# Loading and contracting the first two batches of a batched matmul one by one on all 128 rows

## Chip, cores and metric

One core of a Trainium2 chip. The metric is the time of one execution on the device, in microseconds (us). Each kernel is run several times beside the kernel before on the same chip. A ratio is the mean time of one kernel's fast runs over the mean of the other's fast runs of the same rounds, so it is not quite the ratio of the medians quoted beside it; brackets give its 95% interval. A run counts as slow when it is over 1.5% above the fastest of the same kernel. "MiB complete at t" in my own tables is summed from the packet records of a trace (start, duration and size of each DMA packet), with t counted from the start of the span.

Words used below: PE is TensorE with its matmuls, PEld its loading of weights, DVE is VectorE, ACT is ScalarE, SPq is the issuing of DMAs by SyncE. The span is the profiled execution from its first to its last instruction. A run of bytes is a stretch that lies together in memory; each is moved as one packet. A DMA has landed when the last of the 16 DMA engines has delivered its share. The turn is the moment near 80 us at which the queue goes over from loads to outputs.

## The reference

```python
def setup_inputs():
    batch, m, k, n = 16, 512, 512, 512
    return {"a": np.random.randn(batch, k, m).astype(np.float32),
            "b": np.random.randn(batch, k, n).astype(np.float32)}

def reference(a, b):
    return np.matmul(a.transpose(0, 2, 1), b).astype(np.float32)
```

Sixteen products of 512 x 512 matrices. 33.6 MB are read and 16.8 MB written.

## The kernel before

Batches are taken in pairs. The two batches of a pair lie one above the other in the 128 partitions: partitions 0 to 63 hold batch 0, 64 to 127 batch 1, each partition eight rows of k, so one load is 2 MB in 16 KB runs. Each matmul contracts 64 rows; the two batches run side by side in the two row groups of the array.

```python
G = 2; Q = P // G; R = K // Q; V = 2; RV = R // V; T = M // P; H = T // 2; pairs = batch // G
in_v = [x.rearrange("(pair g) (q r) m -> pair (g q) r m", g=G, r=R) for x in (a, b)]
NX = 4                                    # input buffers of 2 MB
x_ts   = [pool.tile([P, R, M], f32) ...]  # NX of them
abf_ts = [pool.tile([P, RV, M], bf) ...]  # V of them; bbf_ts the same
# ... cut ...
for n in range(2 * pairs):                # SyncE: all loads, then all outputs, one queue
    if n >= NX:
        nc.sync.wait_ge(s_in, n - NX + 1) # a buffer is free when both halves are cast
    nc.sync.dma_start(x_ts[n % NX][:], in_v[n % 2][n // 2]).then_inc(s_x[n % NX], 16)
for i in range(pairs - 1):
    nc.sync.wait_ge(s_out, i + 1)
    nc.sync.dma_start(out_v[i], o_ts[i % NO][:]).then_inc(...)

for i in range(pairs):                    # VectorE: f32 -> bf16, in two halves v
    for v in range(V):
        if i and v == 0: nc.vector.wait_ge(s_v, G * i)
        if i and v == 1: nc.vector.wait_ge(s_mm, G * H * i)
        for n in (2 * i, 2 * i + 1):
            if v == 0: nc.vector.wait_ge(s_x[n % NX], 16 * (n // NX + 1))
            nc.vector.tensor_copy(out=(bbf_ts if n % 2 else abf_ts)[v][:],
                                  in_=x_ts[n % NX][:, v * RV:(v + 1) * RV, :]).then_inc(s_cast, 1)
            if v == V - 1:
                nc.vector.memset(dve_done[:, n:n + 1], 0.0).then_inc(s_in, 1)

with nc.tensor.Fori(0, pairs):            # TensorE
    for v in range(V):
        nc.tensor.wait_ge(s_cast, 2).then_inc(s_cast, -2)
        for t in range(T):
            # ... wait for a free PSUM tile; cut ...
            for r in range(RV):
                for g in range(G):
                    rows = slice(g * Q, (g + 1) * Q)
                    # matmul of 64 rows into ps_ts[g][h]; cut
# ScalarE copies PSUM to o_ts and marks the pair for output; cut
```

Of the kernel before, what the change touches and what calls it, by code (L numbers as in the profile page):

```python
# [1 line left out]

# [4 lines left out]

@with_exitstack
def kernel(
    ctx: ExitStack,  # L10
    tc: tile.TileContext,
    a: bass.AP,
    b: bass.AP,
    out: bass.AP,
):
    nc = tc.nc
    P = 128
    batch, K, M = a.shape
    _, _, N = b.shape
    f32 = mybir.dt.float32  # L20
    bf = mybir.dt.bfloat16




    G = 2
    Q = P // G
    R = K // Q
    V = 2
    RV = R // V  # L30
    T = M // P
    H = T // 2
    pairs = batch // G
    in_v = [x.rearrange("(pair g) (q r) m -> pair (g q) r m", g=G, r=R) for x in (a, b)]
    out_v = out.rearrange("(pair g) (c t) n -> pair c g t n", g=G, t=T)

    NX = 4
    NO = pairs - 1



    pool = ctx.enter_context(tc.tile_pool(name="sb", bufs=1))
    psum = ctx.enter_context(tc.tile_pool(name="ps", bufs=1, space=bass.MemoryType.PSUM))


    done = pool.tile([1, 96], f32, name="done")
    dve_done, act_done = done[:, 0:2 * pairs], done[:, 2 * pairs:3 * pairs]
    x_ts = [pool.tile([P, R, M], f32, name=f"x{j}") for j in range(NX)]
    abf_ts = [pool.tile([P, RV, M], bf, name=f"abf{v}") for v in range(V)]
    bbf_ts = [pool.tile([P, RV, N], bf, name=f"bbf{v}") for v in range(V)]  # L50
    o_ts = [pool.tile([P, G, T, N], f32, name=f"o{j}") for j in range(NO)]
    ps_ts = [[psum.tile([P, 2, N], f32, name=f"ps{g}{h}") for h in range(H)] for g in range(G)]

    s_x = [tc.alloc_semaphore(f"s_x{j}") for j in range(NX)]
    s_o0 = tc.alloc_semaphore("s_o0")
    s_o = tc.alloc_semaphore("s_o")
    s_in = tc.alloc_semaphore("s_in")
    s_cast = tc.alloc_semaphore("s_cast")
    s_v = tc.alloc_semaphore("s_v")
    s_mm = tc.alloc_semaphore("s_mm")  # L60
    s_ev = [tc.alloc_semaphore(f"s_ev{h}") for h in range(H)]
    s_out = tc.alloc_semaphore("s_out")

    with tc.tile_critical(no_gpsimd_drain=True):  # L64
        for n in range(2 * pairs):
            if n >= NX:
                nc.sync.wait_ge(s_in, n - NX + 1)
            nc.sync.dma_start(x_ts[n % NX][:], in_v[n % 2][n // 2]).then_inc(s_x[n % NX], 16)
        for i in range(pairs - 1):
            nc.sync.wait_ge(s_out, i + 1)  # L70
            nc.sync.dma_start(out_v[i], o_ts[i % NO][:]).then_inc(s_o if i else s_o0, 16)

        for i in range(pairs):
            for v in range(V):
                if i and v == 0:
                    nc.vector.wait_ge(s_v, G * i)
                if i and v == 1:
                    nc.vector.wait_ge(s_mm, G * H * i)
                for n in (2 * i, 2 * i + 1):
                    if v == 0:  # L80
                        nc.vector.wait_ge(s_x[n % NX], 16 * (n // NX + 1))
                    nc.vector.tensor_copy(  # L82
                        out=(bbf_ts if n % 2 else abf_ts)[v][:],
                        in_=x_ts[n % NX][:, v * RV:(v + 1) * RV, :],
                    ).then_inc(s_cast, 1)
                    if v == V - 1:

                        nc.vector.memset(dve_done[:, n:n + 1], 0.0).then_inc(s_in, 1)  # L88

        for h in range(H):  # L90
            nc.tensor.sem_inc(s_ev[h], 1)
        with nc.tensor.Fori(0, pairs):
            for v in range(V):
                nc.tensor.wait_ge(s_cast, 2).then_inc(s_cast, -2)
                for t in range(T):
                    h = t // 2
                    if v == 0 and t % 2 == 0:
                        nc.tensor.wait_ge(s_ev[h], 1).then_inc(s_ev[h], -1)  # L98
# [3 lines that stand above are left out]
                            a_m = abf_ts[v][rows, r, :].rearrange("p (c t) -> p t c", t=T)  # L102
                            mm = nc.tensor.matmul(  # L103
                                ps_ts[g][h][:, t % 2, :],
                                a_m[:, t],
                                bbf_ts[v][rows, r, :],
                                start=(v == 0 and r == 0),
                                stop=(v == V - 1 and r == RV - 1),
                            )
                            if v == 0 and t == T - 1 and r == RV - 1:  # L110
                                mm.then_inc(s_v, 1)
                            if v == V - 1 and t % 2 and r == RV - 1:
                                mm.then_inc(s_mm, 1)

        for i in range(pairs):
            if i == NO:
                nc.scalar.wait_ge(s_o0, 16)
            for h in range(H):
                for g in range(G):
                    nc.scalar.wait_ge(s_mm, G * H * i + G * h + g + 1)  # L120
                    ev = nc.scalar.copy(  # L121
                        out=o_ts[i % NO][:, g, 2 * h:2 * h + 2, :], in_=ps_ts[g][h][:]
                    )
                ev.then_inc(s_ev[h], 1)

            nc.scalar.memzero(act_done[:, i:i + 1]).then_inc(s_out, 1)  # L126


    with tc.tile_critical(sync_engine=mybir.EngineType.Pool, no_gpsimd_drain=True):
        nc.gpsimd.wait_ge(s_o0, 16)  # L130
        nc.gpsimd.wait_ge(s_o, 16 * (pairs - 2))
    tc.no_sync_barrier()
    nc.sync.dma_start(out_v[pairs - 1], o_ts[(pairs - 1) % NO][:])


# [1 line left out]
_INS = ['a', 'b']  # L137
_OUTS = [((16, 512, 512), 'float32')]


# [23 lines left out]
```

## Time and profile before

| | |
|---|---|
| time, median of the first 3 runs | 123.9 us (123.84 to 124.15) |
| span of the profiled run | 121.9 us |
| PE, VectorE, ScalarE busy | 51%, 31%, 26% of the span |
| DMA queue busy | 97.6% of 16 engines' span |

How to read it: compare the last row with the one above it.

### The profile page before, as it was taken

The page shows a single profiled execution, that of the slowest core. Times are in us where ns is not written, and L with a number is a line of the kernel's source. Part 1 is how long each engine was busy: PE and PEld are TensorE (multiplying, and loading weights), DVE is VectorE, ACT ScalarE, POOL GpSimd, SP SyncE. Part 2 cuts the span into 40 slices and gives each one's busy share as a digit, 9 for nine tenths or more (in the row PEclk, how much of TensorE's full clock was granted, in tenths as well). Part 3 has the DMA queues.
Part 4 walks back from the last instruction along what each step waited for, and adds up shares of the span by engine and source line. Part 5 has one row for each costly group of instructions (what it writes and reads, how often), then busy time and mean ns, then how long its engine had stood idle before and what let it go on. Part 6 is the DMA issues. An engine that isn't in the chain of part 4 may idle for free. (4 is left out here: it accounts for less than half of the span.)

```text
span 121.9 us, 1261 instructions
## 1 busy us (share of the span) xinstructions
PE 62.5 (51%) x512; PEld 35.8 (29%) x512; DVE 38.0 (31%) x48; ACT 31.8 (26%) x41; POOL 0.2 (0%) x4
## 2 busy tenths in 40 slices
PE   0000099989669749969919988946960000000000
PEld 0000044546246314536605645624630000000000
DVE  0003560784194092474356247419000000000000
ACT  4000000480920830190470075091083000000000
POOL 0000000000000000000000000000000000000000
PEclk9999999999999977999995899999999655555555
DMA  5899999999999999999999999999999999999994
GB/s 108 360 430 430 436 430 430 430 430 430 430 430 430 430 430 436 430 430 430 430 430 430 430 430 430 436 390 428 428 430 430 430 428 430 430 430 428 428 428 175
DMA packets 4480, 50.33 MB, mean 413 GB/s; under 512 B 384, under 2 KB 384, under 8 KB 384
## 3 DMA queue, kind: packets, MB, share of 16 engines
q1 hardware_dynamic: 4480, 50.33, 97.6%
HBM read 33.55 MB, written 16.78 MB: 413 GB/s over the span
## 5 line engine op out<-in xcount | busy, mean ns | idle before, releaser
L103 PE MATMUL ps<-bbf,abf 64*128 64x512 bf16 x512 | 62.5, 403 | 27.9 <-PEq L98 27.9
L103 PEld LDWEIGHTS ps<-bbf,abf 64*128 64x128 bf16 x512 | 35.8, 114 | 54.1 <-issue 37.8
L121 ACT COPY o<-ps 128x1024 f32<-128x1024 f32 x32 | 30.1, 1026 | 59.8 <-PE ps L103 59.8
L82 DVE CAST abf<-x 128x2048 bf16<-128x2048 f32 x16 | 19.6, 1224 | 26.6 <-PE ps L103 17.6
L82 DVE CAST bbf<-x 128x2048 bf16<-128x2048 f32 x16 | 19.6, 1225 | 20.8 <-DMA x<-in_b_dram 20.8
L126 ACT ACTIVATE done<-done 1x1 uint32<-1x1 uint32 x8 | 1.6, 196 | 0.0
L121 ACT ACT_TABLE_LOAD x1 | 1.3, 1283 | 0.9 <-SPq L64 0.9
L88 DVE MEMSET done<- 1x1 f32 x16 | 0.9, 59 | 0.0
L148 POOL MEMSET const-bfloat16-1.0<- 128x1 bf16 x1 | 0.1, 101 | 0.0
L148 POOL MEMSET const-uint8-127<- 128x1 uint8 x1 | 0.1, 101 | 0.0
L148 POOL MEMSET const-float32-0.0<- 128x1 f32 x1 | 0.1, 98 | 0.2 <-issue 0.2
L148 POOL MEMSET const-float32-1.0<- 128x1 f32 x1 | 0.1, 98 | 0.0
## 6 DMA issues: line engine op xcount, KB each, us to landing
x<-in_a_dram SPq DMA_DIRECT2D x8, 2048.0 KB, 12.1
x<-in_b_dram SPq DMA_DIRECT2D x8, 2048.0 KB, 15.9
out_dram<-o SPq DMA_DIRECT2D x8, 2048.0 KB, 30.8
```

The lines of the kernel that those rows point to most:

```text
L82: nc.vector.tensor_copy(out=(bbf_ts if n % 2 else abf_ts)[v][:], in_=x_ts[n % NX][:, v * RV:(v + 1) * RV, :],).then_inc(s_cast, 1)
L88: nc.vector.memset(dve_done[:, n:n + 1], 0.0).then_inc(s_in, 1)
L103: mm = nc.tensor.matmul(ps_ts[g][h][:, t % 2, :], a_m[:, t], bbf_ts[v][rows, r, :], start=(v == 0 and r == 0), stop=(v == V - 1 and r == R ...
L121: ev = nc.scalar.copy(out=o_ts[i % NO][:, g, 2 * h:2 * h + 2, :], in_=ps_ts[g][h][:])
L126: nc.scalar.memzero(act_done[:, i:i + 1]).then_inc(s_out, 1)
L148: nc = _bacc.Bacc("TRN2", target_bir_lowering=False, num_devices=1)
```

## The change

The intent: let PE begin sooner. The first two batches are loaded one after the other, each spread over all 128 partitions (four rows of k per partition, 8 KB runs, 1 MB per DMA), so the first batch is there after half the bytes, and it is contracted on all 128 rows with half as many matmuls. All other pairs stay as they were.

```diff
+    in0_v = [x.rearrange("batch (p r) m -> batch p r m", r=RV) for x in (a, b)]
...
-        for n in range(2 * pairs):
+        for u in range(G):
+            for j in range(2):
+                nc.sync.dma_start(
+                    x_ts[j][:, u * RV:(u + 1) * RV, :], in0_v[j][u]
+                ).then_inc(s_x[j] if u else s_f[j], 16)
+        for n in range(2, 2 * pairs):
...
+        for u in range(G):
+            if u:
+                nc.vector.wait_ge(s_mm, H)               # batch 1's casts wait for batch 0's matmuls
+            for j, bf_ts in enumerate((abf_ts, bbf_ts)):
+                nc.vector.wait_ge(s_x[j] if u else s_f[j], 16)
+                nc.vector.tensor_copy(
+                    out=bf_ts[0][:], in_=x_ts[j][:, u * RV:(u + 1) * RV, :]
+                ).then_inc(s_cast, 1)
+                if u == G - 1:
+                    nc.vector.memset(dve_done[:, j:j + 1], 0.0).then_inc(s_in, 1)
...
+                if i == 1 and v == 0:
+                    nc.vector.wait_ge(s_mm, G * H)       # pair 1's casts wait for batch 1's matmuls
...
+        with nc.tensor.Fori(0, G):
+            a_m = abf_ts[0][:].rearrange("p r (c t) -> p r t c", t=T)
+            nc.tensor.wait_ge(s_cast, 2).then_inc(s_cast, -2)
+            for t in range(T):
+                # ... wait for a free PSUM tile; cut ...
+                for r in range(RV):
+                    mm = nc.tensor.matmul(ps_ts[0][h][:, t % 2, :], a_m[:, r, t], bbf_ts[0][:, r, :],
+                                          start=(r == 0), stop=(r == RV - 1))
+                if t % 2:
+                    mm.then_inc(s_mm, 1)
-        with nc.tensor.Fori(0, pairs):
+        with nc.tensor.Fori(0, pairs - 1):
```

(ScalarE's copies of the first pair change their order accordingly.)

More of the change, by code (lines that the diff above doesn't have):

```diff
@@ L54 @@
     s_x = [tc.alloc_semaphore(f"s_x{j}") for j in range(NX)]
+    s_f = [tc.alloc_semaphore(f"s_f{j}") for j in range(2)]
     s_o0 = tc.alloc_semaphore("s_o0")
@@ L71 @@
             nc.sync.dma_start(out_v[i], o_ts[i % NO][:]).then_inc(s_o if i else s_o0, 16)
-        for i in range(pairs):
-            for v in range(V):
-                if i and v == 0:
-                    nc.vector.wait_ge(s_v, G * i)
-                if i and v == 1:
+        for u in range(G):
[8 more added lines that the diff above has]
+                    nc.vector.memset(dve_done[:, j:j + 1], 0.0).then_inc(s_in, 1)
+        for i in range(1, pairs):
+            for v in range(V):
+                if i == 1 and v == 0:
+                    nc.vector.wait_ge(s_mm, G * H)
+                if i > 1 and v == 0:
+                    nc.vector.wait_ge(s_v, G * (i - 1))
+                if i > 1 and v == 1:
                     nc.vector.wait_ge(s_mm, G * H * i)
@@ L91 @@
             nc.tensor.sem_inc(s_ev[h], 1)
-        with nc.tensor.Fori(0, pairs):
+        with nc.tensor.Fori(0, G):
+            a_m = abf_ts[0][:].rearrange("p r (c t) -> p r t c", t=T)
+            nc.tensor.wait_ge(s_cast, 2).then_inc(s_cast, -2)
+            for t in range(T):
+                h = t // 2
+                if t % 2 == 0:
+                    nc.tensor.wait_ge(s_ev[h], 1).then_inc(s_ev[h], -1)
+                for r in range(RV):
+                    mm = nc.tensor.matmul(
+                        ps_ts[0][h][:, t % 2, :],
+                        a_m[:, r, t],
+                        bbf_ts[0][:, r, :],
+                        start=(r == 0),
+                        stop=(r == RV - 1),
+                    )
+                if t % 2:
+                    mm.then_inc(s_mm, 1)
+        with nc.tensor.Fori(0, pairs - 1):
             for v in range(V):
@@ L117 @@
                 nc.scalar.wait_ge(s_o0, 16)
-            for h in range(H):
+            if i == 0:
+                for g in range(G):
+                    for h in range(H):
+                        nc.scalar.wait_ge(s_mm, H * g + h + 1)
+                        nc.scalar.copy(
+                            out=o_ts[0][:, g, 2 * h:2 * h + 2, :], in_=ps_ts[0][h][:]
+                        ).then_inc(s_ev[h], 1)
+            for h in range(H if i else 0):
                 for g in range(G):
```

## The prediction

> **What bounds the kernel now.** I read the page first: the table of busy time, the forty slices, the queue.
>
> ```profile
> PE 62.5 (51%) x512; PEld 35.8 (29%) x512; DVE 38.0 (31%) x48; ACT 31.8 (26%) x41; POOL 0.2 (0%) x4
> ...
> DMA  5899999999999999999999999999999999999994
> GB/s 108 360 430 430 436 430 430 430 430 430 430 430 430 430 430 436 430 430 430 430 430 430 430 430 430 436 390 428 428 430 430 430 428 430 430 430 428 428 428 175
> ...
> q1 hardware_dynamic: 4480, 50.33, 97.6%
> ```
>
> No compute engine is busy for much over half of the span, while the DMA row reads 9 from the third slice to the last but one and GB/s stays at 430. The kernel is one long transfer: 50.33 MB / 430 GB/s = 117.0 us of the 121.9 us span. The rest lies at both ends and at the turn from reading to writing, so I cut those into half microseconds (columns: stretch, length, busy time of the engines, clock, DMA share, GB/s).
>
> ```profile
> 1.50:2.00 0.50, 0.00 (x0) 0.00 (x0) 0.00 (x0) 0.50 (x1) 0.00 (x0) 1.00 0.48 131
> 2.00:2.50 0.50, 0.00 (x0) 0.00 (x0) 0.00 (x0) 0.18 (x1) 0.00 (x0) 1.00 1.74 295
> 2.50:3.00 0.50, 0.00 (x0) 0.00 (x0) 0.00 (x0) 0.00 (x0) 0.00 (x0) 1.00 0.80 164
> 3.00:3.50 0.50, 0.00 (x0) 0.00 (x0) 0.00 (x0) 0.00 (x0) 0.00 (x0) 1.00 0.52 164
> 3.50:4.00 0.50, 0.00 (x0) 0.00 (x0) 0.00 (x0) 0.00 (x0) 0.00 (x0) 1.00 0.69 295
> ...
> 80.50:81.00 0.50, 0.14 (x2) 0.00 (x0) 0.00 (x0) 0.50 (x2) 0.00 (x0) 1.00 0.47 197
> ...
> 120.00:120.50 0.50, 0.00 (x0) 0.00 (x0) 0.00 (x0) 0.00 (x0) 0.00 (x0) 0.50 0.25 98
> ```
>
> Five terms: 1.5 us before the first packet; a ramp from 1.5 to 4.0 us that moves 0.52 MB where 430 GB/s would move 1.07, a loss of 1.28 us; 117.0 us of bytes; 0.27 us lost in the dip at 80.5 us; about 1.7 us from the last packet (120.2) to the end. Sum 121.8, against 121.9 measured. The timed 123.9 us is 2.0 us over the span. No compute appears in the sum. It matters only if it starves the queue, so the next view is the instructions in order of time, first those of the queue's issuer, then those of VectorE and of PE.
>
> ```profile
> 0.94 0.39 SPq L68 DMA_DIRECT2D x<-in_a_dram  x1
> 1.39 0.42 SPq L68 DMA_DIRECT2D x<-in_b_dram  x1
> 1.86 0.42 SPq L68 DMA_DIRECT2D x<-in_a_dram  x1
> 2.32 0.69 SPq L68 DMA_DIRECT2D x<-in_b_dram  x1
> 16.08 0.33 SPq L68 DMA_DIRECT2D x<-in_a_dram  x1
> 17.23 0.33 SPq L68 DMA_DIRECT2D x<-in_b_dram  x1
> 26.07 0.33 SPq L68 DMA_DIRECT2D x<-in_a_dram  x1
> ```
>
> ```profile
> 8.84 1.23 DVE L82 CAST abf<-x 128x2048 bf16<-128x2048 f32 x1 [8.84 <-DMA x<-in_a_dram]
> 13.67 1.23 DVE L82 CAST bbf<-x 128x2048 bf16<-128x2048 f32 x1 [3.60 <-DMA x<-in_b_dram]
> 14.81 1.22 DVE L82 CAST abf<-x 128x2048 bf16<-128x2048 f32 x1
> ...
> 15.19 9.54 PE L103 MATMUL ps<-bbf,abf 64*128 64x512 bf16 x64 [15.19 <-PEq L98]
> ...
> 23.44 1.23 DVE L82 CAST bbf<-x 128x2048 bf16<-128x2048 f32 x1 [0.87 <-DMA x<-in_b_dram]
> ```
>
> The fifth load is issued at 16.08, while the first four still run: b of pair 1 lands only at 23.44. Unhindered, a load lands 2.0 MB / 430 = 4.88 us after the one before it, so the fifth is due at 28.3; the very first load took 8.84 - 0.94 = 7.9 us from issue to landing on an empty queue. Issued by 28.3 - 7.9 = 20.4 it leaves no gap: slack 4.3 us. For the seventh the limit is 20.4 + 9.75 = 30.1; it is issued at 26.07, slack 4.0. These are the quantities on which the change could act. At the other end the last output is issued at 92.71 and the queue runs on to 120.2; compute leads by 27 us there (the issuer's longest wait, 27.8 us, is for the output DMA).
>
> The chain of waits in the page ends at the last ScalarE mark and covers about 7% of the span; it misses the DMA tail, so I do not use it.
>
> **What the Trainium skill says.** "DMA: Bandwidth & Descriptors", section Bandwidth ("Where 436 GB/s comes from"), gives a port ceiling of 435 GB/s for the sixteen engines; the trace agrees with its 430, so there is nothing to win in rate. The same page, "Rules for kernel authors", asks for 128 partitions and at least 1 MiB per DMA; the new loads are just that. "TensorE: Matmul & The Clock Gate", Part 1, says that the array starts at half clock and is released after some 3.4 us of activity. The trace shows it: weight loads come in twos 0.427 us apart from 15.16 to 20.24, and later 64 matmuls take 7.21 us, 0.225 us a pair. Its Part 2 says that a weight load for the next matmul is pulled ahead of the running one if it goes to another row group or to the background weight buffer. The kernel before alternates between two row groups, so its trace cannot tell what full-array loads will do; that is my main uncertainty below.
>
> **The change, part by part.**
> Loads. Two 2 MB loads become four of 1 MB, in 8 KB runs instead of 16 KB. Bytes are the same. Each DMA carries 16 tiny packets (the page has 384 under 512 B for 24 DMAs), so packets go from 4480 to 1792 + 512 for inputs, 2048 for outputs and 26 x 16 = 416 small ones: 4768. If the whole gap from 435 to 430 (1.1% of 117 us, 1.35 us) were the price of 24 DMAs, one would cost 0.056 us, and two more 0.1 us. Outputs already go in 8 KB runs, at 430 GB/s from 93 to 105 us, so the shorter run should cost no rate. Two more issues of about 0.45 us lie before the data that they fetch is needed. Net: 0 to +0.1 us.
>
> First compute. Half of each 2 MB comes 2.44 us sooner: a of batch 0 at 8.84 - 2.44 = 6.4, b of batch 0 at 8.84, a and b of batch 1 at 11.3 and 13.7. PE starts 1.52 us after the b landing (15.19 - 13.67), so at 10.4 instead of 15.2. This gain of 4.8 us is not on the path that sets the end; no output is issued before 66.27 in any case.
>
> New waits. There is only one pair of bf16 buffers for both batches, so the casts of batch 1 wait for all 16 matmuls of batch 0, and the casts of pair 1 wait for all of batch 1. Batch 0: 16 matmuls of 128 rows, about 12 cold at 0.427 (5.1 us of cold clock, as before) and 4 at 0.225: 6.0 us, to 16.4. Cast of a of batch 1 then starts near 16.5, and the fifth load comes 1.27 us later (16.08 - 14.81): 17.8, against the limit of 20.4. Its slack falls from 4.3 to 2.6 us and stays positive. The other cast ends near 19.0, PE restarts at 19.1 and, warm, takes 16 x 0.225 = 3.6 us, to 22.7. Pair 1's casts: a from 22.8, b from 24.0, second a from 25.1, so the seventh load at 26.4 (26.07 before), limit 30.1. PE takes up pair 1 at 25.3 (25.10 before). From there both kernels are alike.
>
> Matmuls fall from 512 to 480, worth some 32 x 0.11 us of PE time in the first pair at most; PE is not on the path. ScalarE copies keep their number and size.
>
> Sum: 121.9 + 0.05 in the span, hence 123.9 timed.
>
> **The rivals.**
> (1) The queue runs dry. If full-array weight loads (0.11 us each in the trace) do not hide, batch 0 takes 1.8 us more and ends at 18.2: fifth load at 19.6, still under 20.4; batch 1 ends at about 26.3 and the seventh load goes at 30.0, right at its limit. If moreover the clock drops in the pause between the batches (2.7 us; the trace shows pauses of 2.3 to 2.7 us, with 64 matmuls in 7.10 after the one at 80.6 to 83.3, so still warm), batch 1 costs another 3 us, and the gap in the queue is about 3 us: 127. Both must hold together; I give that 3%. One alone makes 0 to 0.5 us.
> (2) The earlier start of compute is worth its 4.8 us: 119. It would need compute on the path at the end. The 27 us between the last output's issue and its landing speak against it. 1%.
> (3) The ramp changes. The loss of 1.28 us belongs to the first packets, 16 KB each; packets of 8 KB could shorten or lengthen it by some tenths. Nothing in the profile tells the sign. 123.5 to 124.3.
> (4) Reads in 8 KB runs are slower than writes in 8 KB runs. At 390 GB/s, the rate of the worst full slice, 4.19 MB would take 1.0 us more: 124.9. I see no ground for it.
>
> **Range and chances.** The centre is 123.9. Runs of before spread over 0.3 us, and (3) and a little of (4) add some tenths on either side, more upwards because of (1): 123.5 to 124.5. Over 2% faster means under 121.4, which only (2) gives: 0.01. Over 2% slower means over 126.4, which only the full form of (1) gives: 0.03. Within 2%: 0.96.
>
> **What would show it right or wrong.** Right: GB/s at 430 in every slice from the third to the last but one except near 80 us; 4768 packets; first cast at about 6.4 and first matmul near 10.4 us; fifth load issued near 17.8 and seventh near 26.4; last output issued near 92.7 as before; span within 0.4 us of 121.9. Wrong: a slice near 23 or 33 us with less than 400 GB/s would be rival 1; a first stretch with another shape, rival 3; landings of the first four loads more than 2.44 us apart, rival 4; a last output that lands sooner by as much as compute starts sooner, rival 2.

## The result, and the profile after

Changed kernel 124.14 us (median of 4, 124.02 to 124.19), kernel before 123.92 us (median of 4): ratio 1.0013 [0.9996, 1.0031]. A second set on another occasion gave 123.97 against 124.11, ratio 0.9995 [0.9974, 1.0016]. No difference can be told.

The page of the changed kernel:

```profile
PE 64.9 (53%) x480; PEld 35.8 (29%) x480; DVE 37.9 (31%) x48; ACT 32.1 (26%) x41; POOL 0.2 (0%) x4
...
DMA  2999999999999999999999999999999999999994
GB/s 56 423 429 429 458 429 434 434 429 429 429 429 440 429 434 429 429 429 429 429 429 429 429 429 429 429 332 429 426 429 426 429 429 426 429 429 429 429 429 169
...
q1 hardware_dynamic: 4768, 50.33, 97.4%
```

The picture is the one of before: the queue is full from the second slice to the last but one, with a dip at the turn to writing, and 4768 packets as counted ahead. Now the order of time, with the same columns as before (start, length, instruction, wait):

```profile
0.94 0.39 SPq L71 DMA_DIRECT2D x<-in_a_dram  x1
...
5.88 1.23 DVE L87 CAST abf<-x 128x2048 bf16<-128x2048 f32 x1 [5.88 <-DMA x<-in_a_dram]
8.31 1.23 DVE L87 CAST bbf<-x 128x2048 bf16<-128x2048 f32 x1 [1.20 <-DMA x<-in_b_dram]
...
9.83 5.78 PE L121 MATMUL ps<-bbf,abf 128*128 128x512 bf16 x16 [9.83 <-PEq L119]
...
15.65 1.23 DVE L87 CAST abf<-x 128x2048 bf16<-128x2048 f32 x1 [6.12 <-PE ps L121]
...
16.93 0.33 SPq L77 DMA_DIRECT2D x<-in_a_dram  x1
...
18.33 4.96 PE L121 MATMUL ps<-bbf,abf 128*128 128x512 bf16 x16 [2.71 <-PEq L119]
...
21.18 1.63 PEld L121 LDWEIGHTS ps<-bbf,abf 128*128 128x128 bf16 x8 [0.19 <-issue]
...
25.98 7.10 PE L141 MATMUL ps<-bbf,abf 64*128 64x512 bf16 x64 [2.70 <-PEq L136]
...
26.87 0.33 SPq L77 DMA_DIRECT2D x<-in_a_dram  x1
...
83.62 9.89 PE L141 MATMUL ps<-bbf,abf 64*128 64x512 bf16 x64 [3.40 <-PEq L136]
...
95.82 0.37 SPq L178 DMA_DIRECT2D out_dram<-o  x1
```

PE starts at 9.83 instead of 15.19 us. The fifth load, formerly issued at 16.08, now goes at 16.93, the seventh at 26.87 (26.07 before), and PE takes up pair 1 at 25.98 instead of 25.10: the head start of 5.4 us is used up by the two added waits before the second pair begins. Even the last output, issued at 95.82 instead of 92.71 (its matmuls ran at half clock at first, 9.89 us instead of 7.10), makes no difference, since the queue still has outputs to write until 121 us.

Where in the queue do the small differences lie? My sums of completed packets, in us:

```
MiB complete             1      4     30     32     last packet ends
before                 5.82  13.11  76.32  81.19   120.62
before, second trace   5.80  13.09  76.30  81.13   120.66
changed                5.42  12.87  76.09  81.66   121.00
changed, second trace  5.41  12.77  75.98  81.58   120.93
```

The changed kernel's queue is 0.4 us ahead at 1 MiB, 0.2 to 0.3 us ahead through the reading, and 0.3 to 0.5 us behind after the turn to writing. In these traces the changed kernel is left 0.3 to 0.4 us behind, as in the spans (122.3 and 122.2 us against 121.9 twice). The timed runs do not tell this from nothing: their intervals hold 1.

### The profile page after: what moved, and what is told of

Its sections match the earlier page's. It is cut to its first block, busy times and chain, and to the rows that moved or that the text cites. A ratio compares the mean times of both kernels' runs of the same rounds, so it can differ in the third digit from the quotient of the medians.

```text
span 122.3 us, 1205 instructions
## 1 busy us (share of the span) xinstructions
PE 64.9 (53%) x480; PEld 35.8 (29%) x480; DVE 37.9 (31%) x48; ACT 32.1 (26%) x41; POOL 0.2 (0%) x4
## 2 busy tenths in 40 slices
DMA packets 4768, 50.33 MB, mean 412 GB/s; under 512 B 416, under 2 KB 416, under 8 KB 416
## 3 DMA queue, kind: packets, MB, share of 16 engines
q1 hardware_dynamic: 4768, 50.33, 97.4%
## 5 line engine op out<-in xcount | busy, mean ns | idle before, releaser
L141 PE MATMUL ps<-bbf,abf 64*128 64x512 bf16 x448 | 54.2, 400 | 16.0 <-PEq L136 16.0
L141 PEld LDWEIGHTS ps<-bbf,abf 64*128 64x128 bf16 x448 | 31.8, 113 | 38.5 <-issue 24.3
L121 PE MATMUL ps<-bbf,abf 128*128 128x512 bf16 x32 | 10.7, 509 | 12.5 <-PEq L119 12.5
L121 PEld LDWEIGHTS ps<-bbf,abf 128*128 128x128 bf16 x32 | 4.0, 130 | 18.8 <-issue 17.8
## 6 DMA issues: line engine op xcount, KB each, us to landing
out_dram<-o SPq DMA_DIRECT2D x8, 2048.0 KB, 31.7
```

The costliest lines, as they stand in the source:

```text
L121: mm = nc.tensor.matmul(ps_ts[0][h][:, t % 2, :], a_m[:, r, t], bbf_ts[0][:, r, :], start=(r == 0), stop=(r == RV - 1),)
L141: mm = nc.tensor.matmul(ps_ts[g][h][:, t % 2, :], a_m[:, t], bbf_ts[v][rows, r, :], start=(v == 0 and r == 0), stop=(v == V - 1 and r == R ...
```

## The experiments

The theory: the end is set by the bytes in the queue; compute lies beside it, and it can only do harm, namely if it makes a load go out after its limit (20.4 us for the fifth, 30.1 for the seventh). Main rival: the start of compute moves the end.

### The changed kernel again (r1_after_again)

No edit.

> The changed kernel once more, for a tighter interval and a second trace. Queue theory (the end is set by the bytes in the queue alone, compute lies beside it): ratio 1.000 to 1.003; the first megabyte of loads is complete some 0.35 us sooner than in the kernel before (first packets of 8 KB instead of 16 KB), 0.16 us of that is lost again over the first 4 MB (0.309 us for an 8 KB packet against 0.611 for 16 KB), and the rest is decided at the turn from reading to writing near 80 us, which took 0.5 us more in the first trace. If that turn is chance, it differs here; if it belongs to the change, the slice at 79 to 82 us shows about 330 GB/s again. Rival (compute that starts 5 us sooner moves the end): ratio 0.96.

Measured: 123.97 us against 124.11, 0.9995 [0.9974, 1.0016]. The 0.4 us head start at 1 MiB is there again, and so is the longer turn (5.60 us from 30 to 32 MiB, 5.57 in the first trace). The rival's 0.96 is excluded.

### The loads alone (split_only)

```diff
+        for v in range(V):
+            for j in range(2):
+                nc.sync.dma_start(x_ts[j][:, v * RV:(v + 1) * RV, :],
+                                  in_v[j][0][:, v * RV:(v + 1) * RV, :]
+                                  ).then_inc(s_x[j] if v else s_f[j], 16)
+        for n in range(2, 2 * pairs):
```

(and VectorE waits for each half; compute as in the kernel before.)

> The loads alone: the first pair in four 1 MB DMAs of 8 KB runs, all compute as in the kernel before (two row groups, both batches together). Queue theory: the same head start of the queue as in the changed kernel (0.35 us at 1 MB, 0.2 us at 4 MB), first matmul near 9.8 us, fifth load issued near 12 us, time 123.6 to 124.0. If the 0.2 us by which the changed kernel was slower came from the two additional DMAs or the shorter runs, it shows here too: 124.1 or more. If it came from the compute part, this run is 123.9 or less. Rival, compute start sets the end: 119.

Measured: 124.16 us against 124.11, 1.0007 [0.9987, 1.0026].

```profile
10.15 9.95 PE L111 MATMUL ps<-bbf,abf 64*128 64x512 bf16 x64 [10.15 <-PEq L106]
...
12.35 0.33 SPq L74 DMA_DIRECT2D x<-in_a_dram  x1
```

PE started at 10.15 us and the fifth load went at 12.35, 3.7 us sooner than in the kernel before; the time did not move. At 1 MiB the queue was 0.3 us ahead, and the turn took 5.27 us. The edit holds the early PE start without the added waits, so an early start is worth nothing by itself. At 124.16 the median is on the "124.1 or more" side of what I had set down, but the interval holds 1, so it decides nothing about two DMAs more.

### The compute part alone (array_only, array_only2)

```diff
-        for u in range(G):
-            for j in range(2):
-                nc.sync.dma_start(
-                    x_ts[j][:, u * RV:(u + 1) * RV, :], in0_v[j][u]
-                ).then_inc(s_x[j] if u else s_f[j], 16)
+        for j in range(2):
+            nc.sync.dma_start(
+                x_ts[j][:].rearrange("p (u r) m -> p u (r m)", u=G),
+                in0_v[j][0:G].rearrange("u p r m -> p u (r m)"),
+            ).then_inc(s_x[j], 16)
```

(and VectorE's first two casts wait for the whole load; the rest is the changed kernel.)

> The compute part alone: the first pair in two 2 MB DMAs (8 KB runs), both batches landing together, then batch by batch on the full array with the one pair of bf16 buffers. Queue theory with its limit of 20.4 us for the fifth load: b lands near 13.3, first matmul near 14.8, batch 0 done near 20.6, so the fifth load is issued near 21.9, 1.5 us too late; the seventh goes near 32, about at its limit of 30.1 + 1.5. The queue runs dry for 1.2 to 2 us near 23 us, time 125.2 to 126.0, ratio 1.010 to 1.017. Rival (the time follows the start of compute, which is as in the kernel before): 123.9.

Measured: four fast runs of 126.06 to 126.53 us, ratio 1.0173 [1.0146, 1.0199], just above what was expected (125.2 to 126.0, 1.010 to 1.017). Three more runs were 2 to 3 us longer still (128.5 to 129.3) and count as slow; the profiled one is among them, so from its trace I read only the stretch that explains the fast runs too. Issue and rate around the fifth load, columns of the second fence as in the prediction:

```profile
22.06 0.33 SPq L76 DMA_DIRECT2D x<-in_a_dram  x1
...
32.03 0.33 SPq L76 DMA_DIRECT2D x<-in_a_dram  x1
```

```profile
20.00:22.00 2.00, 0.75 (x4) 0.17 (x2) 1.21 (x3) 1.01 (x1) 0.00 (x0) 1.00 1.09 467
22.00:23.00 1.00, 0.00 (x0) 0.00 (x0) 1.00 (x3) 0.00 (x0) 0.00 (x0) 0.93 0.20 82
23.00:24.00 1.00, 0.55 (x2) 0.29 (x3) 0.16 (x2) 0.00 (x0) 0.00 (x0) 0.50 1.39 262
24.00:25.00 1.00, 1.00 (x4) 0.29 (x2) 0.00 (x0) 0.00 (x0) 0.00 (x0) 0.50 0.72 262
25.00:26.00 1.00, 1.00 (x4) 0.32 (x3) 0.00 (x0) 0.00 (x0) 0.00 (x0) 0.50 0.99 426
```

The queue ran dry at 22 us. From 8 to 10 MiB it took 6.43 us instead of 4.86, so 1.57 us were lost, and the load had gone out at 22.06: the limit is 22.06 - 1.57 = 20.5 us, against 20.4 predicted. From 12 to 14 MiB another 0.6 us went (seventh load at 32.03, limit 30.1 + 1.57 = 31.7). Together 2.2 us, which is what the fast runs are longer by (126.3 - 124.1); that a fast run has these same holes is argued, since no trace of one was taken. The load that went out into the dry queue landed at 29.73, 7.7 us after its issue, against the 7.9 on which the prediction's limit rests. So the compute part is harmless only because the 1 MB loads come with it.

> The compute part alone once more, because the first trace fell in a slow run. In the trace of a fast run the queue should be late by 1.5 to 1.6 us at 10 MB and by some 2.3 us from 14 MB on (fifth load near 22.1 against its limit of 20.5; then the seventh near 32.0), and by nothing more than a few tenths at the turn: span near 124.3, time 126.0 to 126.4.

Three of four runs were slow again (128.3 to 129.2), one fast (126.09), the trace slow. The trace repeats the loss of 1.64 us from 8 to 10 MiB; its turn took 6.11 us, not the few tenths more that I had set down. What makes the slow mode stays open; that kernel fell into it in 6 of 11 runs. The landing records of both slow traces show one thing of it: up to the sixth load the 16 engines deliver within 0.9 us of one another, from the seventh, the second late one, 1.9 and 2.7 us apart, and they stay apart to the end, without any instruction fetch (see below) in either trace. Whether the fast runs are free of this, no trace shows.

### Matmuls of the first two batches two and three times (mm_x2, mm_x3)

```diff
-            for t in range(T):
-                h = t // 2
-                if t % 2 == 0:
+            for w in range(2 * T):                 # 3 * T in mm_x3
+                t, rep = w % T, w // T
+                h = t // 2
+                if t % 2 == 0 and rep == 0:
...
-                if t % 2:
+                if t % 2 and rep == 2 - 1:         # 3 - 1 in mm_x3
```

> The changed kernel with the sixteen matmuls of each of the first two batches run twice (same result, PE busy longer). The run with the compute part alone gave the limit: fifth load at 22.06 us, queue 1.57 us late, so limit 20.5, here 20.3 because the queue is 0.2 us ahead. Queue theory: batch 0 ends near 19.0, fifth load near 20.3, gap 0 to 0.3; batch 1 ends near 30.1, seventh load near 33.6 against a limit of 30.1, gap 3.5; time 127.0 to 128.2. Rival (the queue has more buffered than I think, or compute in the head never matters): 124.

> The same with the matmuls three times. Queue theory: batch 0 ends near 22.5, fifth load near 23.8, gap 3.5; batch 1 ends near 36.9, seventh load near 40.4 against 33.5, gap 6.9; time 133.5 to 135.5, so that from the second to the third dose each microsecond of a late load is a microsecond of the end. Rival: 124, or an increase well under the lateness of the loads.

Measured: mm_x2 127.95, 127.83 and 129.54 us (fast), one slow; 1.039 [1.033, 1.046]. mm_x3 134.37, 134.73 and 134.23 us (fast), two slow; 1.0863 [1.0843, 1.0883]. The rate row of mm_x2 (a slice is 3.2 us):

```profile
GB/s 88 415 418 444 436 426 462 400 421 431 161 379 431 436 426 421 436 431 441 426 426 431 431 431 441 379 361 428 431 423 428 434 421 431 431 423 426 431 400 21
```

Its fifth load went at 20.34, at the limit, and no hole is seen there; the seventh went at 32.39, 2.3 us after the limit, and the slice at 32 us falls to 161 GB/s; 12 to 14 MiB took 2.4 us too long. In mm_x3 (trace of a slow run) the fifth went at 24.23, 3.9 us late, and 8 to 10 MiB lost 4.2 us; the seventh at 41.28, 7.0 us late, and 12 to 14 MiB lost 7.1. Within each trace the holes are as long as the loads are late, to 0.3 us: the mechanism is shown at three doses (array_only, mm_x2, mm_x3). The limits used here are 20.3 us for the fifth load (20.5 from array_only, less the 0.2 by which this queue is ahead; the prediction said 20.4) and, for the seventh, the predicted 30.1 plus the hole before it.

The totals are another matter. mm_x3 fell within 133.5 to 135.5; of mm_x2 two fast runs fell within 127.0 to 128.2 and one above. From the second to the third dose the fast runs grew by 6.0 us (means of 128.4 and 134.4), but the holes of the two traces by 8.9 us. So the forecast of a microsecond at the end for each microsecond of late load is not shown: the fast runs of mm_x3 are only some 10.5 us longer than the changed kernel, less than the 11.3 us of holes in its slow trace, and their own holes must be smaller (their mean granted clock was 0.872 to 0.886, in the slow runs 0.858 to 0.860; no fast trace was kept). And the totals carry something else: the trace of mm_x2 shows a 16 KB instruction fetch at 39.99 us, that of mm_x3 one at 47.4, and by the landing records one engine then trails the others to the end (by 1.0 us in mm_x2, 1.6 in mm_x3); see the next two experiments.

### Own bf16 buffers for batch 1 (own_buffers)

```diff
-            if u:
-                nc.vector.wait_ge(s_mm, H)
...
-                    out=bf_ts[0][:], in_=x_ts[j][:, u * RV:(u + 1) * RV, :]
+                    out=bf_ts[u][:], in_=x_ts[j][:, u * RV:(u + 1) * RV, :]
...
-        with nc.tensor.Fori(0, G):
-            a_m = abf_ts[0][:].rearrange("p r (c t) -> p r t c", t=T)
+        for u in range(G):                          # written out, buffer u
+            a_m = abf_ts[u][:].rearrange("p r (c t) -> p r t c", t=T)
```

> The changed kernel with the second, unused pair of bf16 buffers for batch 1, so that its casts no longer wait for the matmuls of batch 0. Queue theory: fifth load issued near 12 us instead of 16.9, batch 1's matmuls directly behind batch 0's, and none of it in the end: ratio 0.998 to 1.002. Rival (the wait that the change added costs something, or an earlier fifth load helps): 0.5% or more faster.

Measured: 126.15 us against 123.8, 1.0183 [1.0167, 1.0199]. Neither theory had this. The fifth load did go at 12.02 and batch 1 followed batch 0 without a gap. But the page has a line that the changed kernel's lacks:

```profile
q1 hardware_dynamic: 4768, 50.33, 96.0%
q8 instruction: 1, 0.02, 0.0%
```

One packet of instructions, 16 KB, in flight from 33.36 us for 0.93 us by the packet records. The Trainium skill, "Runtime: NRT & Kernel Launch", section "Instruction fetch mechanics", says that each engine's instruction memory is refilled in 16 KiB blocks by DMA while it runs, and calls the cost "mostly hidden". No trace of a kernel with a shorter PE program has this line; the four with a longer one (this, the next, mm_x2 and mm_x3) all have it. Writing the loop out put 16 more matmuls into PE's program; that was a side effect of my edit, and the next run has it alone.

### The loop written out, nothing else (unroll_only)

```diff
-        with nc.tensor.Fori(0, G):
+        for _ in range(G):
```

> The changed kernel with nothing altered but that PE's loop over the first two batches is written out (16 more matmuls in PE's program; buffers, waits and order as in the changed kernel). The run with its own buffers for batch 1, which had to write the loop out too, was 1.8% slower against all expectation, and its page shows one 16 KB transfer on an instruction queue at 33 us, after which one of the 16 engines delivers every load 1.2 to 1.3 us after the others, to the end. If that fetch is the cause: the same line on the page here, the same straggler, time 125.4 to 126.4, ratio 1.012 to 1.02. If the cause is the early fifth load or the removed wait: no such line, 124.0, ratio 1.000 to 1.002.

Measured: 125.94 us against 123.99, 1.0152 [1.0138, 1.0166]. The line is there again:

```profile
q1 hardware_dynamic: 4768, 50.33, 96.1%
q8 instruction: 1, 0.02, 0.0%
```

and a cast that in the changed kernel waited for PE (37.91 us) now waits for its load:

```profile
32.57 1.23 DVE L103 CAST bbf<-x 128x2048 bf16<-128x2048 f32 x1 [1.90 <-DMA x<-in_b_dram]
...
38.82 1.23 DVE L103 CAST abf<-x 128x2048 bf16<-128x2048 f32 x1 [2.74 <-DMA x<-in_a_dram]
```

Each load is split over 16 engines and has landed when the last of them is done. By the landing records (unroll_only, us):

```
landing of load (last engine)        27.7   32.5   38.7   43.6   58.1   77.5   84.0   (output)  123.2
last engine behind the one before    0.05   0.01   1.32   1.30   1.25   1.20   2.02             1.99
```

The fetch starts at 32.62 us and lasts 0.93; the next load has one straggler 1.3 us behind, and it is still behind at the end. Why it never catches up is not shown; it would follow if every engine had a fixed share of each transfer. The end shows it (half-empty engines in the last stretches; first unroll_only, then the changed kernel):

```profile
120.00:121.00 1.00, 0.00 (x0) 0.00 (x0) 0.00 (x0) 0.00 (x0) 0.00 (x0) 0.50 0.36 148
121.00:122.00 1.00, 0.00 (x0) 0.00 (x0) 0.00 (x0) 0.00 (x0) 0.00 (x0) 0.50 0.08 33
122.00:123.00 1.00, 0.00 (x0) 0.00 (x0) 0.00 (x0) 0.00 (x0) 0.00 (x0) 0.50 0.04 16
```

```profile
120.00:121.00 1.00, 0.00 (x0) 0.00 (x0) 0.00 (x0) 0.00 (x0) 0.00 (x0) 0.50 0.45 188
121.00:122.00 1.00, 0.00 (x0) 0.00 (x0) 0.00 (x0) 0.00 (x0) 0.00 (x0) 0.50 0.00 0
```

In unroll_only a tail at 33 and 16 GB/s, which is about one engine's share (430 / 16 = 27), goes on for 2 us after the others are done. The other 15 engines end the last output at 121.25 us, as in the changed kernel (121.30), so the loss is the lag of one engine: 1.3 us from the first load after the fetch, and 0.7 us more that it gained at the turn, for a reason that stays open. A lag can also arise without a fetch (1.4 us in the slow trace of array_only, from its second hole on); here it begins with the fetch, in both kernels that have the loop written out.

So writing out a loop of 16 matmuls cost 1.5%, and of the 1.8% of own_buffers some 0.3% is left for everything else in it; taking the wait away gained nothing.

### The kernel before once more (before_again)

No edit.

> The kernel before once more, for a second trace. The traces so far differ at the turn from reading to writing: the two megabytes from 30 to 32 MB took 4.87 us in the kernel before, 5.57 and 5.60 in two traces of the changed kernel, 5.27 with the loads alone split. If the turn is chance, it takes 5.2 to 5.7 here; if it belongs to the change, 4.9 again. Ratio 0.998 to 1.002 in both cases.

Measured: 123.97 us against 123.8, 1.0022 [0.9998, 1.0046]. The turn took 4.83 us (4.87 in the first trace). So of what I set down, "chance" failed: two traces of before have 4.8 to 4.9, two of the changed kernel 5.6. But two traces each do not settle it: unroll_only, whose loads and waits are those of the changed kernel, took 5.36, small_first, which is the kernel before but for its first load, 5.09, and own_buffers 5.98. Why, I do not know. In all of them some 16 KB packets shortly before the turn take 0.9 us or more instead of 0.611: 1 to 3 from 78 us on in the kernel before, 21 and 22 of some 65 in the changed one. It costs 0.7 us, against which the head start of 0.4 us stands.

### Small runs first (small_first)

```diff
+            if n == 0:
+                for lo, hi in ((0, 1), (1, 2), (2, 4)):        # runs of 2, 2 and 4 KB
+                    nc.sync.dma_start(x_ts[0][:, lo:hi, :], in_v[0][0][:, lo:hi, :]).then_inc(s_f, 16)
+                nc.sync.dma_start(x_ts[0][:, RV:, :], in_v[0][0][:, RV:, :]).then_inc(s_x[0], 16)
+                continue
```

> The kernel before with only its very first load cut into 2 KB, 2 KB, 4 KB and 8 KB runs (four DMAs), the rest in 16 KB runs. If each engine's first packets are slow in proportion to their size (in the trace of before they take 0.8 to 1.9 us instead of 0.611, in the changed kernel 0.3 to 1.2 instead of 0.309), the queue is 0.35 to 0.6 us ahead at 1 MB and keeps most of it, since later packets are 16 KB: time 123.4 to 123.7, ratio 0.995 to 0.998. If the slow start is a fixed time or the small runs cost as much as they win: 123.9 or more.

Measured: 124.44 us against 124.11, 1.0040 [1.0013, 1.0066]: a miss. At 0.5 MiB the queue was 0.3 us ahead of before (4.29 against 4.60), but at 1 MiB 0.14 behind and at 3 MiB 0.37 behind. Its 2 KB packets took 0.084 us each, 10% more than an eighth of a 16 KB packet (0.611 / 8 = 0.076), and that accounts for only 0.1 us; the rest I cannot place. These smaller first runs gained nothing, so no version faster than both came out of this.

### 8 KB runs everywhere (runs8_1mb, runs8_2mb)

```diff
 # runs8_1mb
-            nc.sync.dma_start(x_ts[n % NX][:], in_v[n % 2][n // 2]).then_inc(s_x[n % NX], 16)
+            for v in range(V):
+                nc.sync.dma_start(
+                    x_ts[n % NX][:, v * RV:(v + 1) * RV, :], in_v[n % 2][n // 2][:, v * RV:(v + 1) * RV, :]
+                ).then_inc(s_x[n % NX] if v else s_f[n % NX], 16)
 # runs8_2mb: two batches side by side in a partition; the result is wrong on purpose
+    in0_v = [x.rearrange("(pair g) (p r) m -> pair p g (r m)", g=G, r=R // G) for x in (a, b)]
-            nc.sync.dma_start(x_ts[n % NX][:], in_v[n % 2][n // 2])
+            nc.sync.dma_start(x_ts[n % NX][:].rearrange("p (g r) m -> p g (r m)", g=G), in0_v[n % 2][n // 2])
```

> The kernel before with every input load as two 1 MB DMAs of 8 KB runs (right result; 40 DMAs instead of 24). From the packet times (0.309 us for 8 KB, 0.611 for 16 KB) each pair of short packets costs 0.007 us more; 128 per engine make 0.9 us; the 16 additional DMAs at an estimated 0.056 us at most another 0.9; the short first packets win 0.35. Time 124.4 to 125.3, ratio 1.004 to 1.011. Rival (run length and number of DMAs are free): 123.9 or less.

> The kernel before with every input load as one 2 MB DMA of 8 KB runs, two batches side by side in each partition while the compute is left as it was (so the result is wrong on purpose; timing only). Same run length as the last run, but 24 DMAs. If the price is the packet's, as the packet times say: 124.4 to 124.7, ratio 1.004 to 1.006. If it is the DMA's: 123.6 to 123.9, and the last run above it by all of the difference.

Measured: 124.09 and 123.98 us against 124.07; 0.9997 [0.9983, 1.0012] and 0.9994 [0.9978, 1.0010]. Both misses: the times do not move. The queue does, inside:

```
MiB complete        1      4     30     32     last packet ends
before            5.82  13.11  76.32  81.19   120.62
1 MB, 8 KB runs   5.42  12.83  76.61  81.54   121.05
2 MB, 8 KB runs   5.40  12.75  76.45  81.35   120.75
```

From 4 to 30 MiB the 8 KB runs took 63.7 to 63.8 us instead of 63.2, so the dearer packets are real (0.5 us); the head start of 0.4 us pays for them. Thirteen of the sixteen additional DMAs lie in that stretch and cost 0.08 us there (63.78 against 63.70), far below the 0.056 us each that I had allowed at most.

## Why the prediction was right, point by point

- **The queue bounds the kernel; 121.8 us in five terms.** Held. The full slices of the changed kernel read 429 GB/s, and with the start of compute moved by 5 us the time stayed (the change itself; split_only, 1.0007) or grew with what happened in the queue: holes in mm_x2 and mm_x3, one trailing engine in unroll_only and own_buffers. Two of the five terms were misread: the view by stretches books a packet where it starts. By the packet records the first data packet starts at 1.96 us, not 1.5, and the last ends at 120.62, not 120.2. Both shifts are some 0.4 us, one makes the head longer, the other the tail shorter, so the sum came out by luck. The span grew by 0.3 to 0.4 us, not 0.05: at the edge of what the prediction allowed, and no more than the timed runs can tell.
- **The limits of 20.4 and 30.1 us.** Held: array_only puts the first at 20.5, mm_x2 the second at 30.0 (32.39 less a hole of 2.4), and at three doses the hole is as long as the load is late. This is the part to learn from: the time from issue to landing on an empty queue (7.9 us before; 7.7 and 7.8 us for the late fifth loads of array_only and mm_x3), taken from the landing that would come in turn.
- **First cast 6.4, first matmul 10.4.** They came at 5.88 and 9.83, because the first packets of 8 KB were sooner through than those of 16 KB (rival 3, which I had left without a sign: 0.4 us at 1 MiB, and 0.4 again in both runs with 8 KB runs everywhere).
- **Fifth load 17.8, seventh 26.4.** 16.93 and 26.87, slack 3.5 and 3.2 us. That the seventh is so near is partly luck: batch 1 began 0.8 us sooner than predicted and then took 1.4 us longer. Full-array weight loads hide: eight in 1.63 us, 0.2 us apart, the distance of the matmuls. That was my main uncertainty, and it is settled.
- **"Warm, 16 x 0.225 = 3.6 us" for batch 1.** Failed: 4.96 us. After the pause of 2.71 us the array ran at half clock again until 21.2 us. I had taken pauses of 2.3 to 2.7 us for harmless because one case in the trace of before was; the same trace has two others where 64 matmuls take 8.59 and 8.79 us after 2.67 us. In unroll_only the same batch took 3.62 us after the same pause of 2.71, so either can happen. It cost 1.4 us of a slack of 4.
- **Price of 8 KB runs and of two DMAs, 0 to 0.1 us.** About right in sum and wrong in its parts: the runs cost a little (about 0.5 us in 26 MiB), the DMAs hardly anything.
- **The turn.** The prediction took it as unchanged; it took 0.7 us longer in both traces of the changed kernel. This is the main open point, at the size of the interval.
- **Last output near 92.7.** 95.82, without effect, as 25 us of outputs were still queued.

## What to carry to other kernels

Where the transfer queue is full from start to end, as here, expect nothing of an earlier start of compute (5 us sooner, no change in time); ask instead for each load at what time it must be issued, and how much of that slack the change uses. Half of a change can be harmful alone and harmless with the other half (here the full-array part without the split loads: 1.7% slower). And look at the list of queues for lines that were not there before: in this kernel, which runs at the pace of the slowest of 16 engines, a written-out loop with one 16 KB fetch of instructions cost 1.5%.

## What the Trainium skill lacked or had wrong

- "Runtime: NRT & Kernel Launch", "Instruction fetch mechanics", calls the cost of crossing a 16 KiB block mostly hidden and says that kernels prefer full unrolling. In this kernel, bound by DMA, it is not hidden: after one fetch of 0.93 us one of 16 engines was 1.3 us behind, 2.0 us after the turn, and the time was 125.94 us against 123.99.
- "DMA: Bandwidth & Descriptors", in its part on the iDMA fabric, says that a bulk load runs at the pace of its slowest engine; it lacks that the lag was not made good on a full queue (1.32 us at 38.7 us, still 1.20 at 77.5 us, 1.99 at the end).
- The same page has no word on the first packets of each engine: mostly 0.8 to 1.9 us for 16 KB where 0.611 is usual, 0.3 to 1.2 for 8 KB where 0.309 is.
- The same page, section "Anatomy of one DMA", gives a fixed cost of some 2 us per DMA, fitted for DMAs issued from GpSimd. It has no figure for one more DMA on a full queue of SyncE: 13 more cost 0.08 us in all.
- "TensorE: Matmul & The Clock Gate", Part 1, names idle windows of about 3.4 us for the return to half clock; here pauses of 2.7 us were followed by half clock in some cases (16 matmuls in 4.96 us) and by full clock in others (the same 16 in 3.62, in unroll_only).
- No page tells how the turn of a queue from loads to stores behaves: 4.8 to 6.0 us in the traces of fast runs for the last 2 MiB of loads where 4.86 is usual.
